# A two-block layer on one core: routing from the unscaled residual, choices by counted ranks, and places of two expert pairs at a time

## The chip, the cores and the metric

The kernel runs on one core of a Trainium2 chip. The metric is the device time of one execution in microseconds (us). TensorE is called PE here, VectorE DVE, ScalarE ACT, GpSimd POOL and SyncE SP; SP issues the weight transfers.

## What is computed

Two blocks on 256 tokens of 1024 fp32 values. The first is an attention layer with a PEER feed-forward part; the change does not touch it. The second is a parallel mixer, a cross-attention to 256 memory rows (weights w_q, w_kv, w_o), a hierarchical mixture of experts and a final norm:

```
def second_block(x, mem, ...):
    x = x + parallel_mixer(rms_norm_2(x, mix_norm[l]), ..., w_out[l])
    x = x + memory_cross_attention(rms_norm_2(x, xattn_norm[l]), rms_norm_2(mem, mem_norm[l]), w_q[l], w_kv[l], w_o[l])
    x = x + hierarchical_moe(rms_norm_2(x, ffn_norm[l]), ...)
    return rms_norm_2(x, final_norm)

def hierarchical_moe(h, w_group, b_group, w_expert, b_expert, w_gate, w_up, w_down):
    g_prob = softmax(t @ w_group + b_group)                     # 4 groups
    g_p, g_idx = lax.top_k(g_prob, 1)
    e_logits = (t @ w_expert + b_expert).reshape(-1, 4, 4)      # 4 experts in each
    e_logits = take_along_axis(e_logits, g_idx[:, :, None], axis=1)[:, 0]
    e_p, e_idx = lax.top_k(softmax(e_logits), 2)
    weights = g_p * e_p / sum(e_p)
    for e in range(16):
        hid = silu(t @ w_gate[e]) * (t @ w_up[e])
        out = out + combine[:, e:e + 1] * (hid @ w_down[e])
```

## The kernel before

Tokens stand in two halves of 128 on the partitions (`xs[0]`, `xs[1]`); `c` is the half. Dense products are made of high and low parts: `unit` (L198, L199) loads a weight tile `raw` and splits it into `whi` (ACT) and `wlo` (DVE), and `mm3` (L206 to L209) multiplies three of the four combinations.

**Cross-attention.** `add_out(yT, w_out2)` ends the mixer, adds to the residual, normalizes it and transposes it; `evac` writes the transposed rows as high and low parts `hq` (L289, L290). w_q, the attention per head, then w_o in two column blocks of 512 (`tok_block`, four units each). The last two units of the second block are done first for half 0, then for half 1 (`tail`).

**Routing.** Behind w_o's second block each half is added (L1239), squared and summed (ACT), scaled by rstd and the gain row into `xl` (L331), transposed (L303), copied to `hT` (L1300) and multiplied with the 20 routing columns (L1303). `split_chunk` (L225, L226) makes `xnh`, `xnl` of `xl`. From the logits `lg` a chain of small DVE operations finds the best group, the best two experts in it (by maxima, with ties broken by rank), and the weights. `M` is the 0/1 table of token to expert. Five matmuls with triangular and all-ones tables (L1377 to L1381) count the tokens ahead of each in its expert, and their totals.

**Places.** Each expert has 64 places. `one_hots` compares the position with 0 to 63 and so makes `Pm`, tokens by places; `gather` multiplies `xnh`, `xnl` with `Pm` and copies the result to `XT` (features by places), 512 places of eight experts at once: one half before the experts, the other (`late`) after the first pair's up and gate products. `back` transposes `Pm` to `PT`, `place_weights` gives each place its weight `cw`.

**Experts.** Two experts at a time, eight pairs `j`. `up_gate` takes eight loads of 1 MB (w_gu), four for the gate, four for up; `down` four (w_dn). `wide` (L1435) issues each load on SP's queue into the ring pool `rawm` of MOE_RAW slots, in which the tiles of w_q and w_o (512 KB each) stand before. SP issues in the order of the program; a load waits until its slot has been read. `to_tokens` puts the outputs back to tokens. If an expert has more than 64 tokens, the whole is repeated for the rest under `If`, by the total `toti` loaded into registers (L1548).

PSUM has four banks `acc` and four `aux`. Outside the listed places the order on the engines is a scheduler's.

Of the kernel before, what the change touches and what calls it, by code (L numbers as in the profile page):

```python
# [9 lines left out]
F32 = mybir.dt.float32  # L10
F32R = mybir.dt.float32r
I32 = mybir.dt.int32
# [10 lines left out]
MOE_RAW = 10  # L23
# [47 lines left out]
def pack(a):  # L71
# [61 lines left out]
    r["ffn"] = _rows(a["ffn_norm_2"][0])  # L133
# [12 lines left out]
def build(tc, I, out):  # L146
# [12 lines left out]
    with es:  # L159
# [201 lines left out]
        xd = dramp.tile([2, 128, D], F32, name="xd")  # L361
# [731 lines left out]
        with ExitStack() as ph:  # L1093
            stream(es, 0, 3, 3)
# [138 lines left out]
            def add_out(aT, src, gain=None, then=None):  # L1233
                tt = Turned(pair("l"))
                for nb in range(2):
                    sl = slice(nb * 512, (nb + 1) * 512)
                    pss = tok_block(aT, src[nb], 8, tail=nb == 1)
                    for c in range(2):
                        V.tensor_add(xs[c][:, sl], pss[c], xs[c][:, sl])  # L1239
                        if nb == 1:  # L1240
                            tt.chunk(xs[c], c, gain)
                            if then is not None:
                                then(tt, c)
                return tt
# [7 lines left out]
            hq = hl_tiles(qp, 8, "hq")  # L1252
# [33 lines left out]
            ffn = tp.tile([128, D], F32, name="ffn", tag="ffn", bufs=1)  # L1286
            SY.dma_start(ffn, I["ffn"])
            wr = qp.tile([128, 160], F32, name="wr")
            br = qp.tile([128, 20], F32, name="br")
            SY.dma_start(wr, I["w_route"])  # L1290
            SY.dma_start(br, I["b_route"])
            lg = small(40, "lg", bufs=1).rearrange("p (a b) -> p a b", a=2)
            hT = qp.tile([128, 8, T], F32, name="hT3", tag="qT")

            def logits(tt, c):
                cs = slice(c * 128, (c + 1) * 128)
                if c == 1:
                    xhl.append(split_chunk(tt.xn[0])[0])
                for q, ps in enumerate(tt.pss):
                    last = S.copy(hT[:, 2 * q:2 * q + 2, cs], ps.rearrange("p (a t) -> p a t", a=2)[:, :, cs])  # L1300
                pl = acc()
                for k in range(8):
                    PE.matmul(pl[:, 0:20], hT[:, k, cs], wr[:, k * 20:(k + 1) * 20], start=k == 0, stop=k == 7)  # L1303
                if c == 0:
                    V.tensor_add(lg[:, c], pl[:, 0:20], br)
                    return
                st["behind"] = (last, st["behind"][1])
                hl, last = split_chunk(tt.xn[1])
                xhl.append(hl)
                with tc.issue_after(last.ins):  # L1310
                    V.tensor_add(lg[:, c], pl[:, 0:20], br)

            xhl = []
            tt = add_out(oT, I["w_o"], ffn, logits)


        with ExitStack() as ph:
# [6 lines left out]
            xn = tt.xn  # L1324
            for c in range(2):
                G.dma_start(xd[c], xn[c])

            rank = mp.tile([128, 4], F32, name="rank")
            for i in range(4):
                V.memset(rank[:, i:i + 1], 4.0 - i)  # L1330
            rk = rank[:, None, :].to_broadcast([128, 2, 4])

            def bc4(m):
                return m.unsqueeze(2).to_broadcast([128, 2, 4])

            def first_max(p, name):
                m = small(2, name + "v")
                V.tensor_reduce(m, p, axis=AX.X, op=OP.max)
                oh = mp.tile([128, 2, 4], F32, name=name)
                V.tensor_tensor(oh, p, bc4(m), op=OP.is_equal)  # L1340
                V.tensor_mul(oh, oh, rk)
                r = small(2, name + "r")
                V.tensor_reduce(r, oh, axis=AX.X, op=OP.max)
                V.tensor_tensor(oh, rk, bc4(r), op=OP.is_equal)
                return oh, m

            def exps(x, m, name):
                p = mp.tile([128, 2, 4], F32, name=name)
                V.tensor_sub(p, x, bc4(m))
                S.activation(p, p, AF.Exp)  # L1350
                return p

            oh, gmax = first_max(lg[:, :, 0:4], "goh")
            gex = exps(lg[:, :, 0:4], gmax, "gex")
            gz = small(2, "gz")
            sel = mp.tile([128, 2, 4, 4], F32, name="sel")
            for c in range(2):
                V.tensor_mul(sel[:, c], lg[:, c, 4:20].rearrange("p (g e) -> p e g", g=4),
                             oh[:, c, None, :].to_broadcast([128, 4, 4]))
            el = mp.tile([128, 2, 4], F32, name="el4")  # L1360
            V.tensor_reduce(el, sel, axis=AX.X, op=OP.add)
            o1, m1 = first_max(el, "eo1")
            ex = exps(el, m1, "ex")
            ex2 = mp.tile([128, 2, 4], F32, name="ex2")
            V.scalar_tensor_tensor(ex2, o1, -4.0, ex, op0=OP.mult, op1=OP.add)
            o2, p2 = first_max(ex2, "eo2")
            V.tensor_add(o1, o1, o2)
# [222 lines left out]
```

## Time and profile before

| | |
|---|---|
| median of 3 runs | 1531.72 us (1527.82 to 1536.29) |
| profiled execution, own time | 1528.59 us |
| its span from first to last instruction | 1526.8 us |
| mean granted clock of PE | 0.942 of 2.4 GHz |
| PE busy over the span | 1255.9 us (82%) |
| DVE / ACT / POOL busy | 1028.4 / 498.5 / 412.4 us |
| moved by DMA | 493.17 MB, mean 323 GB/s |
| expert loads | 96 of 1024 KB, 19.9 us from issue to landing in the middle |

The shares of busy time are means over stages with different limits; the stage of the change is the last 340 us, and there single timelines are read.

### The profile page before, as it was taken

To read this page: it belongs to the slowest core of one execution; us is meant where nothing else is said; L and a number is where in the kernel's file an instruction comes from. 1 tells how busy PE (TensorE), PEld (TensorE's weight loads), DVE (VectorE), ACT (ScalarE), POOL (GpSimd) and SP (SyncE) were. 2 spreads that over 40 slices of the span, in tenths; PEclk is the share of its full clock that TensorE was granted. 3 is DMA by queue.
4 is the path that set the end of the run, shared out by engine and by line. 5 is a ranking of instruction groups with operands and counts; after the bars stand their busy time and mean duration, and the time that the engine had idled before them with its cause. 6 is when DMAs were issued, how large, how long until landed. Compare 5 with 4: busy or idle time off the path is not lost. (4 is left out here: it accounts for less than half of the span.)

```text
span 1526.8 us, 16025 instructions
## 1 busy us (share of the span) xinstructions
PE 1255.9 (82%) x5260; PEld 772.5 (51%) x5260; DVE 1028.4 (67%) x2132; ACT 498.5 (33%) x1001; POOL 412.4 (27%) x306
## 2 busy tenths in 40 slices
PE   7999999999898656666666656767999998998886
PEld 7878787778664222222222222224998875432222
DVE  6899877776878888888988888765896643100002
ACT  5555445754222222222122222213663532100001
POOL 0022000100455666556456565640000000000000
PEclk9999999999999998778899988899999997999999
DMA  8955876364889999999999999996436553999996
GB/s 330 352 204 190 266 275 207 111 247 180 336 354 421 421 420 421 420 420 422 420 421 421 420 420 421 420 421 236 165 111 235 182 207 127 369 420 420 419 420 247
DMA packets 86347, 493.17 MB, mean 323 GB/s; under 512 B 9712, under 2 KB 12528, under 8 KB 39920
## 3 DMA queue, kind: packets, MB, share of 16 engines
q0 software_dynamic: 37152, 269.50, 42.6%
q1 hardware_dynamic: 47088, 219.94, 38.7%
q10 hardware_dynamic: 2016, 2.62, 0.5%
q8 instruction: 44, 0.72, 0.2%
q14 instruction: 47, 0.39, 0.1%
HBM read 487.83 MB, written 4.19 MB: 322 GB/s over the span
## 5 line engine op out<-in xcount | busy, mean ns | idle before, releaser
L981 PE MATMUL acc<-uv,dg 128*128 128x512 f32 x784 | 418.0, 683 | 195.1 <-ACT dg L979 194.9
L944 POOL DMA_INDIRECT uv<-in_uv_dram,ei x256 | 368.7, 1440 | 285.6 <-DMA uv<-in_uv_dram,ei 115.0
L954 DVE CUSTOM_DVE_ANT_0 junk<-uv,h 128x1024 f32<-128x1024 f32 x256 | 313.0, 1223 | 111.1 <-DMA uv<-in_uv_dram,ei 109.3
L981 PEld LDWEIGHTS acc<-uv,dg 128*128 128x128 f32 x784 | 160.7, 215 | 445.4 <-ACT dg L979 277.0
L317 POOL TENSOR_TENSOR rstd<-ms,neghalf 128x1 f32<-128x1 f32 (+3 forms) x38 | 40.2, 1058 | 783.0 <-DVE ms L315 782.9
L199 DVE TENSOR_TENSOR wlo<-raw,whi 128x1024 fp32r<-128x1024 f32 x144 | 174.6, 1219 | 42.8 <-ACT whi L198 37.7
L198 ACT CAST whi<-raw 128x1024 fp32r<-128x1024 f32 x144 | 150.8, 1052 | 122.7 <-PE acc L207 49.0
L959 ACT ACTIVATE ga<-dots 128x2 f32<-128x2 f32 x128 | 26.0, 203 | 382.8 <-DVE dots L954 382.7
L1449 PE MATMUL aux<-raw,XT 128*64 128x512 f32 x512 | 117.6, 599 | 10.5 <-DMA raw<-in_w_gu_dram 10.5
L979 ACT ACTIVATE dg<-ident,wts 128x128 f32<-128x128 f32 x196 | 71.0, 395 | 104.9 <-DVE wts L964 101.9
L206 PE MATMUL acc<-whi,hTh 128*128 128x512 f32 (+1 forms) x240 | 96.6, 405 | 2.2 <-ACT whi L198 1.6
L1456 DVE SCALAR_TENSOR_TENSOR hid<-aux,cw,sgt 128x512 f32<-128x512 f32 x8 | 6.0, 750 | 136.0 <-PE aux L1449 136.0
L207 PE MATMUL acc<-whi,hTl 128*128 128x512 f32 (+1 forms) x240 | 93.4, 392 | 0.0
L1449 PEld LDWEIGHTS aux<-raw,XT 128*64 128x64 f32 x512 | 33.8, 136 | 86.0 <-issue 55.3
L973 DVE SCALAR_TENSOR_TENSOR xl<-uv,wts,xl 128x1024 f32<-128x1024 f32 x58 | 74.5, 1285 | 2.1
L1473 PE MATMUL aux<-raw,hTm 128*64 128x512 f32 x256 | 60.1, 600 | 12.5 <-DMA raw<-in_w_dn_dram 12.0
L209 PE MATMUL acc<-wlo,hTh 128*128 128x512 f32 (+1 forms) x240 | 64.7, 389 | 2.3 <-DVE wlo L199 2.3
L866 PE MATMUL aux<-h2T,uv 128*128 128x256 f32 (+1 forms) x288 | 56.8, 356 | 0.0
L277 DVE TENSOR_TENSOR yl<-aux,yh 128x512 fp32r<-128x512 f32 x16 | 11.1, 691 | 67.4 <-ACT yh L276 67.4
L391 DVE SCALAR_TENSOR_TENSOR ada<-raw,csil,ada 128x1024 f32<-128x1024 f32 x42 | 53.7, 1278 | 0.3 <-DMA raw<-in_w_ada_dram 0.2
L866 PEld LDWEIGHTS aux<-h2T,uv 128*128 128x128 f32 x288 | 49.7, 190 | 7.4 <-issue 1.9
L206 PEld LDWEIGHTS acc<-whi,hTh 128*128 128x128 f32 x240 | 46.0, 192 | 14.5 <-ACT whi L198 3.2
(426 smaller groups left out, 1947.5 us busy)
## 6 DMA issues: line engine op xcount, KB each, us to landing
raw<-in_w_gu_dram SPq DMA_DIRECT2D x64, 1024.0 KB, 19.9
raw<-in_w_dn_dram SPq DMA_DIRECT2D x32, 1024.0 KB, 19.9
raw<-in_w_ada_dram SPq DMA_DIRECT2D x48, 512.0 KB, 4.6
raw<-in_w_qk_dram SPq DMA_DIRECT2D x28, 512.0 KB, 4.6
raw<-in_w_gl_dram SPq DMA_DIRECT2D x16, 512.0 KB, 4.3
uv<-in_w_query_dram SPq DMA_DIRECT2D x8, 1024.0 KB, 9.5
raw<-in_w_out_dram SPq DMA_DIRECT2D x16, 512.0 KB, 4.3
raw<-in_w_v_dram SPq DMA_DIRECT2D x14, 512.0 KB, 4.5
```

Of the source, the lines that this page charges most:

```text
L198: S.copy(hi, raw)
L199: V.tensor_sub(lo, raw, hi.bitcast(F32))
L206: PE.matmul(ps, a[0], b[0], start=first, stop=False)
L207: PE.matmul(ps, a[late], b[1 - late], start=False, stop=False)
L209: PE.matmul(ps, a[1 - late], b[late], start=False, stop=last)
L866: PE.matmul(ps[:, half * w:(half + 1) * w], wq[h][:, j:j + 128], h2T[:, k, cs], start=k == 0, stop=k == 7)
L944: G.indirect_dma_start(out=t, out_offset=None, in_=I["uv"], in_offset=bass.IndirectOffsetOnAxis(ap=ei[:, c, h, k:k + 1], axis=0))
L954: V.tensor_tensor_reduce(junk, fetched[h, c, k][:, 0:D], h2[c], scale=1.0, scalar=0.0, op0=OP.mult, op1=OP.add, accum_out=dots[:, c, h, k: ...
L973: V.scalar_tensor_tensor(part[c], t, w, part[c], op0=OP.mult, op1=OP.add)
L979: S.mul(dg, ident, w)
L981: PE.matmul(vacc[c, i], dg, t[:, i * 512:(i + 1) * 512], start=c not in first, stop=(h, k) == (7, 14 + c))
L1449: PE.matmul(ps[e * 64:(e + 1) * 64], XT[:, k, (2 * j + e) * 64:(2 * j + e + 1) * 64], w[:, (2 * e + i) * 512:(2 * e + i + 1) * 512], start ...
```

## The change

In words: (1) the routing weights are multiplied by the gain column once; the residual itself is transposed and multiplied with them, and rstd is applied to the 20 logits. The first 512 columns of the residual are transposed inside w_o's second block, their logits too. (2) Choices: each logit in a row of four counts those that are greater (or equal, for those ahead of it); rank below 1 for the group and below 2 for the expert gives `M`. The weights are computed later. (3) `xhl`, the high and low parts of the normalized tokens, takes the memory of `hq`; the DRAM copy `xd` goes. (4) `places(q)` works on two pairs (256 places); q = 0 before the experts, 1 to 3 after the downs of pairs 0, 2 and 4. (5) MOE_RAW is 11. (6) The totals move behind the experts. (7) From w_o's second block to the first gather the order on PE, DVE and ACT is the program's, and on PE to the end of the experts.

```diff
-MOE_RAW = 10
+MOE_RAW = 11
...
-            stream(es, 0, 3, 3)
+            stream(ph, 0, 3, 3)
...
-            hq = hl_tiles(qp, 8, "hq")
+            hqp = es.enter_context(pool("hqp", side="right"))
+            hq = hl_tiles(hqp, 8, "hq")
             tt.evac(hq, col("xattn_norm"), None, tp)
             st["raw"] = es.enter_context(pool("rawm", MOE_RAW, side="right"))
...
+            V.tensor_mul(wr, wr, gcol.unsqueeze(2).to_broadcast([128, 8, 20]))
...
+            xhl = [[t.rearrange("p k t -> p (k t)")[:, c * D:(c + 1) * D] for t in hq] for c in range(2)]
...
+            def logits_out(c):
+                V.scalar_tensor_tensor(lg[:, c], pls[c], rs[c], br, op0=OP.mult, op1=OP.add)
+            def highs(c):
+                S.activation(xhl[c][0], xs[c], AF.Copy, scale=rs[c])
+            def lows(c):
+                V.scalar_tensor_tensor(xhl[c][1], xs[c], rs[c], xhl[c][0].bitcast(F32), op0=OP.mult, op1=OP.subtract)
+            for c, po in enumerate(tok_block(oT, I["w_o"][0], 8)):
+                add(c, 0, po)
+                squares(c, 0)
+                turned(c, 0, turn_half(c, 0), S.copy)
+            given.enter_context(tc.manual_schedule(engines={ET.PE, ET.DVE, ET.Activation}))
+            last_o = tok_gen(oT, I["w_o"][1], 8, 512, po.extend, tail=True)
+            for u in range(2):
+                next(last_o)
+            for c in range(2):
+                logits(c, 0)
+            for _ in last_o:
+                pass
...
+            V.tensor_tensor(gt, others_, own, op=OP.is_gt)
+            V.tensor_tensor(ge, others_, own, op=OP.is_ge)
+            V.copy_predicated(gt.rearrange("p r a b -> p r (a b)"), tri[:, None, :].to_broadcast([128, 10, 16]),
+                              ge.rearrange("p r a b -> p r (a b)"))
+            rank = mp.tile([128, 2, 20], F32, name="rank")
+            V.tensor_reduce(rank.rearrange("p c (r f) -> p (c r) f", f=4), gt, axis=AX.X, op=OP.add)
+            oh = mp.tile([128, 2, 4], F32, name="oh")
+            V.tensor_scalar(oh, rank[:, :, 0:4], 0.5, None, op0=OP.is_lt)
...
-            PE.matmul(ps[:, 0:16], before, Mf[:, 0], start=True, stop=True)
-            PE.matmul(ps[:, 16:32], before, Mf[:, 1], start=True, stop=False)
+            PE.matmul(ps[:, 0:32], before, M.rearrange("p c g e -> p (c g e)"), start=True, stop=False)
             PE.matmul(ps[:, 16:32], ones, Mf[:, 0], start=False, stop=True)
-            PE.matmul(ps[:, 32:48], ones, Mf[:, 0], start=True, stop=False)
-            PE.matmul(ps[:, 32:48], ones, Mf[:, 1], start=False, stop=True)
+            lows(0)
...
+            def gather(q):
+                hs = slice(q * 256, (q + 1) * 256)
+                pss = [aux() for _ in range(4)]
+                for p in range(2):
+                    for k, c in ([(k, c) for c in range(2) for k in range(8)] if p == 0 else
+                                 [(k, c) for k in range(8) for c in range(2)]):
+                        PE.matmul(pss[k // 2][:, k % 2 * T:(k % 2 + 1) * T], xhl[c][p][:, k * 128:(k + 1) * 128],
+                                  Pm[:, c, hs], start=c == 0 and p == 0 and k % 2 == 0,
+                                  stop=c == 1 and p == 1 and k % 2 == 1)
...
-                        if which == 0 and u == 1:
+                        if which == 0 and u == 2:
                             between()
...
+                    if j == 0:
+                        place_weights(0)
+                        back(range(2))
...
+                    if j % 2 == 1 and j < 6:
+                        q = (j + 1) // 2
+                        places(q)
+                        place_weights(q)
+                        back(range(2 * q, 2 * q + 2))
```

The order on PE from w_o's last matmuls (L209, changed: L210) to the first expert matmuls (L1449, changed: L1486) was, with the transposes L303, the logits L1303, the counts L1377 to L1381, the gather L1404, and `back` and `place_weights` as L1419 and L1427:

```order
L209 MATMUL acc<-wlo,oTh 128x512 x4
L303 MATMUL aux<-ident,xl 128x128 x8
L1303 MATMUL acc<-wr,hT_8522 128x20 x8
L303 MATMUL aux<-ident,xl 128x128 x8
L1303 MATMUL acc<-wr,hT_8522 128x20 x8
L1377 MATMUL aux<-M,before 128x16
...
L1404 MATMUL aux<-Pm,xnh 128x512
L1404 MATMUL aux<-Pm,xnl 128x512
...
L1419 MATMUL aux<-ident,Pm 128x128 x8
L1427 MATMUL aux<-cx,Pm 128x2 x8
L1449 MATMUL aux<-raw,XT 64x512 x32
```

and is now, with the logits L1328, the transposes of the residual L1313, the counts L1410 and L1411, the gather L1433, `place_weights` L1464 and `back` L1455:

```order
L1328 MATMUL aux<-wr,xT_8523 128x20 x8
...
L210 MATMUL acc<-wlo,oTh 128x512 x4
L1313 MATMUL aux<-ident,x_74 128x128 x4
L1313 MATMUL aux<-ident,x_75 128x128 x4
L1328 MATMUL aux<-wr,xT_8523 128x20 x8
L1410 MATMUL aux<-M,before 128x32
L1411 MATMUL aux<-M,ones 128x16
L1433 MATMUL aux<-Pm,hqh 128x256 x16
L1433 MATMUL aux<-Pm,hql 128x256 x16
L1486 MATMUL aux<-raw,XT 64x512 x12
L1464 MATMUL aux<-cx,Pm 128x2 x4
L1455 MATMUL aux<-ident,Pm 128x128 x4
```

Half of the transposes and logits moved into w_o; `place_weights` and `back` moved behind the third load of the first pair.

The second gather on PE stood between the gate and the up loads of pairs 0 and 1 (32 matmuls of 512 columns, of which two rows are shown):

```order
L1449 MATMUL aux<-raw,XT 64x512 x32
L1404 MATMUL aux<-Pm,xnh 128x512
L1404 MATMUL aux<-Pm,xnl 128x512
...
L1419 MATMUL aux<-ident,Pm 128x128 x8
L1427 MATMUL aux<-cx,Pm 128x2 x8
L1449 MATMUL aux<-raw,XT 64x512 x8
```

and is now the first of three blocks, behind pair 0's down (L1473, changed: L1510):

```order
L1510 MATMUL aux<-raw,hTm 64x512 x16
L1433 MATMUL aux<-Pm,hqh 128x256 x16
L1433 MATMUL aux<-Pm,hql 128x256 x16
L1464 MATMUL aux<-cx,Pm 128x2 x4
L1455 MATMUL aux<-ident,Pm 128x128 x4
L1486 MATMUL aux<-raw,XT 64x512 x12
```

It moved from behind eight loads to behind twenty, with half the columns.

At w_q's start the order on ACT was, with the sums of squares L325, the splits whi of w_q's tiles L198 and the evacuations hqh L289:

```order
L325 ACTIVATE xl,ssq_8064<-x_76 128x512
L198 CAST whi<-raw 128x1024 x2
L289 ACTIVATE hqh<-aux,cols 128x256 x4
L198 CAST whi<-raw 128x1024
L289 ACTIVATE hqh<-aux,cols 128x256 x4
```

and is now (L326, L199 and L290):

```order
L326 ACTIVATE xl,ssq_8063<-x_75 128x512
L290 ACTIVATE hqh<-aux,cols 128x256 x7
L199 CAST whi<-raw 128x1024 x2
L290 ACTIVATE hqh<-aux,cols 128x256
```

Seven of the eight evacuations now stand ahead of w_q's first split.

## Rows read from the trace of the kernel before

**Rows 1.** Stretches: length, busy (instructions) of PE, PEld, DVE, ACT, POOL; PEclk, DMA share, GB/s
```profile
1195.00:1250.00 55.00, 54.97 (x319) 47.81 (x318) 27.82 (x51) 25.14 (x49) 0.00 (x0) 1.00 0.64 224
1260.00:1275.00 15.00, 9.13 (x38) 8.51 (x37) 8.86 (x46) 2.93 (x8) 0.53 (x1) 0.50 0.18 70
1275.00:1285.00 10.00, 9.97 (x54) 8.06 (x55) 3.83 (x8) 4.29 (x7) 0.00 (x0) 0.96 0.01 2
1305.00:1320.00 15.00, 14.97 (x83) 7.19 (x84) 1.78 (x6) 2.52 (x5) 0.00 (x0) 1.00 0.77 287
1320.00:1500.00 180.00, 158.76 (x692) 50.60 (x690) 13.54 (x19) 14.72 (x25) 0.00 (x0) 1.00 1.01 420
```

**Rows 2.** Waits of PE from 1240 us: total us, times, longest
```profile
PE aux L1473 <- DMA raw<-in_w_dn_dram: 12.0, 20, 1.3
```

**Rows 3.** Timeline of SP: start us, us, operation, count
```profile
1163.37 3.76 SPq L179 DMA_DIRECT2D raw<-in_w_q_dram  x8
...
1205.74 40.76 SPq L1435 DMA_DIRECT2D raw<-in_w_gu_dram  x10
...
1286.54 8.91 SPq L1435 DMA_DIRECT2D raw<-in_w_gu_dram  x6
```

**Rows 4.** Timeline of PE, w_o's end to the experts; idle before in brackets
```profile
1251.75 1.07 PE L209 MATMUL acc<-wlo,oTh 128*128 128x512 f32 x4
...
1269.30 0.58 PE L1377 MATMUL aux<-M,before 128*128 128x16 f32 x2 [4.65 <-issue]
...
1272.81 0.79 PE L1404 MATMUL aux<-Pm,xnh 128*128 128x512 f32 x1 [1.22 <-DVE Pm L1392]
...
1275.10 0.63 PE L1404 MATMUL aux<-Pm,xnl 128*128 128x512 f32 x1
1275.53 0.48 PE L1404 MATMUL aux<-Pm,xnh 128*128 128x512 f32 x1
...
1281.44 0.39 PE L1404 MATMUL aux<-Pm,xnl 128*128 128x512 f32 x1
1281.67 1.28 PE L1419 MATMUL aux<-ident,Pm 128*128 128x128 f32 x8
1282.79 1.84 PE L1427 MATMUL aux<-cx,Pm 128*128 128x2 f32 x16
1284.56 5.80 PE L1449 MATMUL aux<-raw,XT 128*64 128x512 f32 x26
```

**Rows 5.** Timeline of DVE in the routing
```profile
1252.69 1.29 DVE L331 SCALAR_TENSOR_TENSOR xl<-x,rstd,ffn 128x1024 f32<-128x1024 f32 x1 [0.73 <-POOL rstd L317]
1253.90 0.68 DVE L1239 TENSOR_TENSOR x<-acc,x 128x512 f32<-128x512 f32 x1
...
1264.69 0.18 DVE L1311 TENSOR_TENSOR lg<-acc,br 128x20 f32<-128x20 f32 x1 [0.66 <-PE acc L1303]
...
1272.06 2.50 DVE L1392 TENSOR_TENSOR Pm<-iota,pos 128x512 fp32r<-128x512 f32 x4
```

**Rows 6.** Timeline of PE around the second half's gather
```profile
1298.45 0.50 PE L1404 MATMUL aux<-Pm,xnh 128*128 128x512 f32 x1
...
1308.88 3.65 PE L1449 MATMUL aux<-raw,XT 128*64 128x512 f32 x16
```

**Rows 7.** Timelines at w_q's start, PE and then ACT
```profile
1181.92 1.07 PE L209 MATMUL acc<-wlo,yTh 128*128 128x512 f32 x4
...
1188.41 0.78 PE L206 MATMUL acc<-hqh,whi 128*128 128x256 f32 x2
...
1187.58 1.69 ACT L289 ACTIVATE hqh<-aux,cols 128x256 fp32r<-128x256 f32 x4 [0.78 <-PE aux L303]
1189.17 1.04 ACT L198 CAST whi<-raw 128x1024 fp32r<-128x1024 f32 x1
```

**Rows 8.** The tile raw from 1130 to 1215 us: from issue to landing
```profile
DMA to landing us min/median/max: 3.4/4.3/11.6
```

**Rows 9.** Timeline of PE at the last down
```profile
1512.11 1.94 PE L1473 MATMUL aux<-raw,hTm 128*64 128x512 f32 x8 [0.50 <-SPq L1552]
```

More of the change, by code (lines that the diff above doesn't have):

```diff
@@ L1313, in build @@
-            xhl = []
-            tt = add_out(oT, I["w_o"], ffn, logits)
+            xT = qp.tile([128, 8, T], F32, name="xT3", tag="qT")
+            sq = [small(2, f"ssqr{c}", bufs=1) for c in range(2)]
+            slot = small(64, "slot", bufs=1)
+            V.tensor_scalar(slot, iota[:, 0:64], -1024.0, None, op0=OP.add)
+            xhl = [[t.rearrange("p k t -> p (k t)")[:, c * D:(c + 1) * D] for t in hq] for c in range(2)]
+            pls = {}
+            tri = small(16, "tri", I32, bufs=1)
@@ new lines, in build, with add, turn_half, squares @@
+            SY.dma_start(tri, I["tri"])
+            def add(c, nb, po):
+                sl = slice(nb * 512, (nb + 1) * 512)
+                V.tensor_add(xs[c][:, sl], po, xs[c][:, sl])
+            def turn_half(c, nb):
+                pt = aux()
+                for i in range(4):
+                    k = 4 * nb + i
+                    PE.transpose(pt[:, i * 128:(i + 1) * 128], xs[c][:, k * 128:(k + 1) * 128], ident)
+                return pt
+            def squares(c, nb):
+                sj = tp.tile([128, 512], F32, name="sj", tag="sj")
+                S.activation(sj, xs[c][:, nb * 512:(nb + 1) * 512], AF.Square, accum_out=sq[c][:, nb:nb + 1])
@@ new lines, in turned, with logits, scale @@
+            def turned(c, nb, pt, copy):
+                copy(xT[:, 4 * nb:4 * nb + 4, c * 128:(c + 1) * 128], pt.rearrange("p (a t) -> p a t", a=4))
+            def logits(c, nb):
+                if nb == 0:
+                    pls[c] = aux()[:, 0:20]
+                cs = slice(c * 128, (c + 1) * 128)
+                for k in range(4 * nb, 4 * nb + 4):
+                    PE.matmul(pls[c], xT[:, k, cs], wr[:, k], start=k == 0, stop=k == 7)
+            rs = []
+            def scale(c):
+                ssq = small(1, "ssq")
+                V.tensor_add(ssq, sq[c][:, 0:1], sq[c][:, 1:2])
+                rs.append(rstd_of(ssq, 1, D))
@@ L1317, in build @@
+            add(1, 1, po[1])
+            turned(0, 1, pt, S.copy)
+            pt = turn_half(1, 1)
+            squares(1, 1)
+            logits(0, 1)
+            turned(1, 1, pt, V.tensor_copy)
+            scale(1)
+            logits(1, 1)
+            highs(0)
+            for c in range(2):
+                logits_out(c)
+            highs(1)
         with ExitStack() as ph:
@@ L1347, in exps @@
[L1347 to L1367, printed above, removed]
+            rows4 = lg.rearrange("p c (r f) -> p (c r) f", f=4)
+            gt = mp.tile([128, 10, 4, 4], F32, name="gt")
@@ new lines, in build @@
+            for c in range(2):
+                one_hots(c, 0)
+            lows(1)
+            st["filled"] = gather(0)
+            m4 = mp.tile([128, 10], F32, name="m4")
+            V.tensor_reduce(m4, rows4, axis=AX.X, op=OP.max)
+            ex = mp.tile([128, 2, 20], F32, name="ex")
+            ex4 = ex.rearrange("p c (r f) -> p (c r) f", f=4)
+            V.tensor_sub(ex4, rows4, m4.unsqueeze(2).to_broadcast([128, 10, 4]))
+            S.activation(ex, ex, AF.Exp)
+            given.close()
```

156 lines of the change are left out of this document (59 added, 97 removed).

## The prediction, made before the changed kernel was run

> **What bounds the kernel now.** I first read the stretches from the memory cross-attention to the end [rows 1]. The reader should look at two columns of them: PE busy and DMA share. From 1195 to 1250 us (w_q, attention, w_o) PE is busy 54.97 of 55 us, so there the bound is PE, and whatever is added to PE's list lengthens the stage. From 1275 to 1285 the DMA share is 0.01: nothing flows. From 1320 to 1500 the share is 1.01 at 420 GB/s while PE is busy 158.76 of 180 us: the expert weights are streamed as fast as they come and PE waits. The waits of PE say the same by name: the largest is 12.0 us for w_dn, in 20 short waits before single loads [rows 2]. A load is 1 MB (128 x 2048 x 4 bytes), so at 420 GB/s one takes 2.5 us.
>
> The timeline of SP says why nothing flows from 1275 to 1285 [rows 3]: ten w_gu loads are issued ahead, into the ten slots of the ring, from 1205.74 to 1246.5; the eleventh goes out at 1286.54. The one PE row that explains this is the first L1449 at 1284.56 [rows 4]: a slot becomes free only when the expert matmuls have read it. So the end of the kernel is the first release, plus 86 remaining loads of 2.5 us, plus every gap in that stream, plus a tail of the last 8 matmuls (1512.11 [rows 9]) and the final norm. A change is worth what it moves of these: the time of the first release, the count of loads behind it, the gaps.
>
> Between w_o's end on PE (1251.75 + 1.07 = 1252.82) and 1284.56 lie 31.7 us [rows 4]. In them PE is idle or on small matmuls, the clock is granted at 0.50 from 1260 to 1275 [rows 1], and the chain is DVE's: the scaled copy of 1.29 us per token half, transposes, logits, the last lg at 1264.69, 29 small routing operations up to 1269.30, five matmuls of counts, positions, four compares Pm in 2.50 us, then 32 gather matmuls, 8 transposes and 8 weight matmuls [rows 4, 5]. The gap is the second half's gather with its transposes, which stands on PE between loads from 1298.45 to 1308.88, 10.4 us [rows 6]; the DMA share from 1305 to 1320 is 0.77 for that [rows 1], because at that time few loads were in flight and no slot was returned.
>
> **The change, part by part.** I call w_o's end on PE E.
>
> Added to w_o's second column block, where PE has no room: 8 transposes and 8 logits matmuls of the first 512 columns. Eight transposes take 1.1 us (1281.67 to 1282.79, 8 rows of L1419 [rows 4]); eight logits matmuls are 16 PE records of a matmul with few columns, and 16 such records of L1427 took 1.8 us (1282.79 to 1284.56 [rows 4]). Sum +3.0 us on E.
>
> The chain after E: residual add 0.68 [rows 5]; 4 transposes 0.6; copy out of PSUM, as wide as the add, 0.7; 4 logits matmuls 0.9; lg 0.2; four hand-overs between engines at about 0.2. That is E + 3.9. The routing is then 8 operations in place of 29. No row of before has a 160-element compare: the lower bound is a small operation, which I put at 0.2 us (29 of them took the 4.4 us up to 1269.30, and some overlap), the upper one half of a 512-wide Pm (2.50 / 4) and a fixed part, 0.36. I take 1.9 us for all 8 (bounds 1.6, all 0.2 apart, and 2.9, all 0.36). Two count matmuls in place of five: 1269.30 to about 1271.6 for five is 0.46 each, so 0.9. Position 0.2, two Pm of half the width 0.7, hand-overs 0.3. First gather matmul at E + 7.9. The STT of 1.28 us that makes the low part of half 0 lies beside the count matmuls, that of half 1 beside the first 16 gather matmuls, which read high parts only; if this cover were gone, it would cost 1.3 each. A gather matmul of 512 columns is 0.43 apart at half clock (1275.10 to 1275.53) and 0.23 at full clock (1281.44 to 1281.67 [rows 4]); half as wide, 0.215 and 0.117. All 32 at half clock take 6.9 us, all at full clock 3.8; I take 5.0, since in before 2.7 us passed (1272.81 to 1275.53) until the faster pitch came. No transposes and no weight matmuls stand before the first expert matmul any more. First expert matmul at E + 12.9 against E + 31.7: −18.8 us.
>
> Moved without being named in the diff's words: the first w_q load. The hq tiles move to a pool of their own ahead of the ring on the right side, the ring gets one slot more, and the first slot then lies over memory that w_out2's stage still uses. In the built program that load waits for w_out2's last matmul (1181.92 + 1.07 = 1183.0 [rows 7]); in before it went out at 1163.37 [rows 3]. SP is in order, so all eight w_q loads go with it, and the scheduler puts seven hqh evacuations ahead of the first whi on ScalarE. Landing took 3.4 us at least, 4.3 in the middle, 11.6 at most [rows 8]; a whi is 1.04 [rows 7]. Lower bound 0: ScalarE is with the evacuations until about 1190.5 anyway. Upper bound 1183.0 + 11.6 + 1.04 − 1188.41 (first w_q matmul [rows 7]) = +7.3. I take +2.5: seven evacuations of 0.42 from 1187.58 on [rows 7], then whi, puts the first matmul at 1191.6, 3.1 late, of which the matmuls then win some back, as in before they started in fits.
>
> So the first release moves by 3.0 + 2.5 − 18.8 = −13.3 us.
>
> Ring of 11: one load fewer behind the first release, 85 in place of 86: −2.5 us. This holds as the eleventh load finds about 20 us without traffic before it.
>
> Places in quarters: the blocks on PE between loads become 32 matmuls of 256 columns (3.8), 4 weight matmuls (8 records, 0.9), 4 transposes (0.6), and about 1 us of waiting for yl and PSUM, b = 6.3 us each, three of them; the first comes after pair 0's down, when six or more loads are in flight. Six loads are 15 us of traffic, so the stream doesn't stop: the gap of before goes, 15 × (1 − 0.77/1.01) = −3.5 us (bounds 0 and −4). PE pays for it from its slack: 95 loads × 1.74 us (8 loads from 1284.56 to 1298.45 [rows 4, 6]) + 8 turns × 0.6 (four transposes) + 6 to_tokens × 1.9 (eight matmuls of 512 columns, 0.23 apart) + 1.6 for pair 0 = 182.7 + 3b, against 3.7 (the first load's matmuls, and about 2 until transfers flow) + 85 × 2.5 = 216 us for the stream. PE takes over as the bound from b = 11 on.
>
> Costed at nothing: the removed xd copies (POOL's queue, nobody waits), the totals and their register load moved to the end (on PE two small matmuls behind the first load of the last down, on SP behind the last weight load), the exps and weights (under the gather; needed only at pair 0's hid). The new small tri load is issued early. If the totals did stand in the tail they would cost about 1 us.
>
> One rule weighs against the price of a load. The rows show 420 GB/s over 180 us [rows 1]. The Trainium skill, "DMA: Bandwidth & Descriptors", section "Where 436 GB/s comes from", says that HBM to SBUF transfers are bound by the HBM side at about 358 GB/s per core; by that a load would take 2.9 us and the sum would be 0.4 us better. The trace does not agree here, and the rows decide.
>
> **Sum.** −13.3 − 2.5 − 3.5 = −19.3 us against the profiled execution's 1528.59: 1509.3. The median of the three runs shown, 1531.72, is 3.1 above that execution, so on that footing 1512.4. I say 1511.
>
> **The rivals.**
> R1, the late w_q loads cost their upper bound: the eight loads start together and the first is slow to land; +4.8 on the forecast, 1516. For it: up to 11.6 us seen; against it: the median of 4.3, and that only one to two loads are needed at once. Chance 0.12.
> R2, the other side: PE becomes the bound through the three blocks. Place: after the downs of pairs 0, 2 and 4. Price 3 × (b − 11) us; it is slower than before from 3 (b − 11) > 19.3, b = 17.5. Against it: the double block of before took 10.4 [rows 6]; for it: a block now waits for yl, Pm and four PSUM banks in turn. At b = 19 it is 1511 + 24 = 1535. Chance 0.03.
> R3, PE stays at 1.2 GHz through routing, gather and into the experts, because the new chain keeps PE idle until E + 7.9 and the gather is short: +1.9 in the gather, +0.9 in logits, +1.7 on the first expert load, and +1 at w_q's start: +5, 1516. For it: 0.50 from 1260 to 1275 [rows 1]; against it: 0.96 in the next ten us, after only 2.7 us of gather at half speed. The Trainium skill, "TensorE: Matmul & The Clock Gate", section "What's actually happening", says that the throttled state is the default and activity releases it, which would go with R3; the trace agrees as to the drop. Chance 0.12.
> R4, the chain does not shorten: something (a PSUM bank of the four, the tri tile, a slot of the hq pool) holds the gather until where it was. Then −18.8 falls away, and +5.5 − 6.0 stays: 1528 to 1531. Against it: each of these is released before w_o ends in the listed order. Chance 0.05.
> The forecast: 0.68.
>
> **How the numbers follow.** The likeliest case goes from 1504 (no loss at w_q, full clock in the gather, the profiled run's footing) to 1516. R1 and R3 together reach 1521. The range 1502 to 1522 leaves out R4, R2 and their mixtures, under 0.2. A measurement of this kernel tells about 0.5%, 7.7 us; faster by more than that means under 1524. Forecast, R1 and R3 are (0.92, less 0.03 for mixtures): faster 0.89; R4 and mixtures: same 0.08; R2: slower 0.03.
>
> **What would show it.** First w_q load on SP at about 1183 and the first w_q matmul 2 to 4 us later than 1188.4; w_o's last matmul at about 1258; first gather matmul 8 us and first expert matmul 13 us behind it, near 1271; eleven w_gu loads before it, then a DMA share of 1.0 without a dip until 1490; three groups of 32 narrow matmuls, each with what follows under 7 us on PE; last 8 matmuls near 1493. It is wrong if PE shows no waits for loads in the middle (R2), if the share dips after the first downs, or if the gap from w_o's end to the experts is over 16 us.

## The result and the profile after

The changed kernel takes 1508.76 us (median of 4 runs, 1507.45 to 1509.14) against 1529.77 us of the kernel before (4 runs beside it): ratio 0.986, 95% interval 0.9837 to 0.9882. The profiled execution has a span of 1505.6 us, 21.2 less than before's 1526.8. The forecast of 1511 lies 2 us off.

Both profiles can be compared from w_out2's last product on; what lies ahead of it is the same work and moved by 0.75 us between them. The marks of the two, in us:

| | before | changed | difference | forecast |
|---|---|---|---|---|
| w_out2's end to the first products of keys and q | 13.41 | 15.41 | +2.0 | +2.5 |
| from there to w_o's end E | 56.42 | 59.80 | +3.4 | +3.0 |
| E to the first gather matmul | 19.99 | 7.41 | −12.6 | −12.1 |
| first gather matmul to first expert matmul | 11.75 | 5.80 | −6.0 | −6.8 |
| first expert matmul to first load into a freed slot | 1.98 | 1.98 | 0 | 0 |
| that load to the end of the last expert matmul | 227.51 | 219.19 | −8.3 | −6.0 |
| from there to the end of the span | 12.75 | 12.27 | −0.5 | 0 |
| sum, from w_out2's end | 343.81 | 321.86 | −21.95 | −19.4 |

(The forecast's column adds to −19.4, the prediction's sum to −19.3; that is rounding.) The rows behind them. The first products of keys and q, in before (L1267) and in the changed kernel (L1266):

```profile
1196.40 0.60 PE L1267 MATMUL aux<-kT,qT 128*128 128x256 f32 x2
...
1199.15 0.60 PE L1266 MATMUL aux<-kT,qT 128*128 128x256 f32 x2
```

PE's timeline of the changed kernel (start, duration, line, operation, count, idle before) from w_o to the experts, and the first block of places between the loads:

```profile
1251.51 1.86 PE L1328 MATMUL aux<-wr,xT 128*128 128x20 f32 x16
1253.21 0.49 PE L207 MATMUL acc<-whi,oTh 128*128 128x512 f32 x1
...
1257.88 1.07 PE L210 MATMUL acc<-wlo,oTh 128*128 128x512 f32 x4
...
1264.52 0.61 PE L1410 MATMUL aux<-M,before 128*128 128x32 f32 x2 [2.27 <-issue]
...
1266.36 3.75 PE L1433 MATMUL aux<-Pm,hqh 128*128 128x256 f32 x16 [0.83 <-DVE Pm L1422]
1269.91 2.32 PE L1433 MATMUL aux<-Pm,hql 128*128 128x256 f32 x16
1272.16 5.37 PE L1486 MATMUL aux<-raw,XT 128*64 128x512 f32 x24
...
1309.02 1.12 PE L1433 MATMUL aux<-Pm,hqh 128*128 128x256 f32 x6
...
1315.35 5.37 PE L1486 MATMUL aux<-raw,XT 128*64 128x512 f32 x24 [0.24 <-ACT PT L1457]
```

L1328 ahead of w_o's last matmuls is the first half of the logits: 1.7 us until the next row, in a stage in which PE is full. Against [rows 4] the reader should see three stretches: from the end of w_o (1257.88 + 1.07) to the counts at 1264.52, 5.6 us, where it took 16.5 in before (1252.82 to 1269.30); the gather, whose first 16 matmuls take 3.55 us and the last 16 only 2.25; and nothing between the gather and 1272.16, the first expert matmul. The block from 1309.02 to 1315.35 is the 6.3 us that the forecast called b. The timeline of SP, which answers to [rows 3]:

```profile
1183.81 3.75 SPq L180 DMA_DIRECT2D raw<-in_w_q_dram  x8
...
1205.77 45.02 SPq L1472 DMA_DIRECT2D raw<-in_w_gu_dram  x11
...
1274.14 8.82 SPq L1472 DMA_DIRECT2D raw<-in_w_gu_dram  x5
```

Eleven loads are issued ahead of the experts. Then the first freed slot is filled at 1274.14, 12.4 us sooner than at 1286.54. The w_q loads go out at 1183.81, right behind w_out2's last product, whereas before they went out 20 us ahead of it. On PE that looks so, to be read with [rows 7]:

```profile
1182.67 1.07 PE L210 MATMUL acc<-wlo,yTh 128*128 128x512 f32 x4
...
1191.72 0.58 PE L207 MATMUL acc<-hqh,whi 128*128 128x256 f32 x1 [3.03 <-ACT whi L199]
```

The stretches, to be read with [rows 1] (length, busy of PE, PEld, DVE, ACT, POOL with counts, clock, DMA share, GB/s):

```profile
1265.00:1270.00 5.00, 4.17 (x20) 4.09 (x20) 2.71 (x5) 0.00 (x0) 0.00 (x0) 0.50 0.05 20
...
1275.00:1280.00 5.00, 5.00 (x30) 2.37 (x28) 0.93 (x4) 0.37 (x1) 0.00 (x0) 1.00 0.97 326
...
1310.00:1315.00 5.00, 4.64 (x40) 4.37 (x38) 2.22 (x6) 1.96 (x5) 0.00 (x0) 1.00 1.01 421
...
1320.00:1480.00 160.00, 148.70 (x706) 58.11 (x704) 17.21 (x32) 17.47 (x32) 0.00 (x0) 1.00 1.01 419
```

The clock is at 0.50 in the five us of the gather's first part, as it was from 1260 to 1275 in before. From 1275 on the DMA share is 1.0, also in the stretch of the first block (1310 to 1315); the 0.77 of before is gone. PE's waits for loads, which were 12.0 us for w_dn [rows 2], have shrunk too:

```profile
PE aux L1510 <- DMA raw<-in_w_dn_dram: 5.0, 9, 0.7
```

That is under half of before's: PE, which has the blocks of places now in this time, is later at the loads. At the end it is PE that comes last:

```profile
1481.23 1.94 PE L1510 MATMUL aux<-raw,hTm 128*64 128x512 f32 x8 [0.57 <-DMA raw<-in_w_dn_dram]
...
1487.96 5.37 PE L1510 MATMUL aux<-raw,hTm 128*64 128x512 f32 x24
```

The last wait for a load is at 1481.23; the last down, of which 1487.96 is the second to fourth load, runs without one, where before's last load was waited for until 1512.11 [rows 9].

### The profile page after: what moved, and what is told of

Read it like the earlier page. It is cut to its first block, busy times and chain, and to the rows that moved or that the text cites. A ratio compares the mean times of both kernels' runs of the same rounds, so it can differ in the third digit from the quotient of the medians.

```text
span 1505.6 us, 16139 instructions
## 1 busy us (share of the span) xinstructions
PE 1257.6 (84%) x5322; PEld 778.5 (52%) x5322; DVE 1029.3 (68%) x2128; ACT 500.8 (33%) x1003; POOL 411.0 (27%) x304
## 5 line engine op out<-in xcount | busy, mean ns | idle before, releaser
L981 PE MATMUL acc<-uv,dg 128*128 128x512 f32 x784 | 430.1, 702 | 185.3 <-ACT dg L979 185.3
L981 PEld LDWEIGHTS acc<-uv,dg 128*128 128x128 f32 x784 | 166.2, 222 | 442.3 <-ACT dg L979 264.8
L199 ACT CAST whi<-raw 128x1024 fp32r<-128x1024 f32 x144 | 150.9, 1053 | 126.2 <-PE acc L208 51.5
L1486 PE MATMUL aux<-raw,XT 128*64 128x512 f32 x512 | 114.9, 597 | 6.4 <-DMA raw<-in_w_gu_dram 4.3
L1486 PEld LDWEIGHTS aux<-raw,XT 128*64 128x64 f32 x512 | 35.0, 137 | 78.9 <-issue 61.7
L210 PE MATMUL acc<-wlo,hTh 128*128 128x512 f32 (+1 forms) x240 | 64.6, 389 | 2.2 <-DVE wlo L200 2.2
L1510 PE MATMUL aux<-raw,hTm 128*64 128x512 f32 x256 | 58.7, 598 | 5.1 <-DMA raw<-in_w_dn_dram 5.0
L210 PEld LDWEIGHTS acc<-wlo,hTh 128*128 128x128 f32 x240 | 43.5, 188 | 12.0 <-DVE wlo L200 2.7
```

What stands on the lines that cost most here:

```text
L199: S.copy(hi, raw)
L210: PE.matmul(ps, a[1 - late], b[late], start=False, stop=last)
L981: PE.matmul(vacc[c, i], dg, t[:, i * 512:(i + 1) * 512], start=c not in first, stop=(h, k) == (7, 14 + c))
L1486: PE.matmul(ps[e * 64:(e + 1) * 64], XT[:, k, (2 * j + e) * 64:(2 * j + e + 1) * 64], w[:, (2 * e + i) * 512:(2 * e + i + 1) * 512], start ...
```

## The experiments

The 1180 us ahead of the stage differ between executions and chips by several us (runs of the kernel before: 1524 to 1537), so edits worth 2 us are read in two ways: by medians beside the changed kernel on one chip where there is one, and by the profile from w_out2's end, as in the table above. The changed kernel was profiled three times: 321.86 us, 323.79 (`changed_again`) and 321.78 (`changed_third`). What made the second longer is the clock: w_o's end comes 1.35 us later behind w_out2's, and the gather lasts 6.38 us in place of 5.80 (the low stretches at w_q's start are shown below).

**The late load.** Edit:

```diff
+            st["raw"] = es.enter_context(pool("rawm", MOE_RAW, side="right"))
             hqp = es.enter_context(pool("hqp", side="right"))
             hq = hl_tiles(hqp, 8, "hq")
             tt.evac(hq, col("xattn_norm"), None, tp)
-            st["raw"] = es.enter_context(pool("rawm", MOE_RAW, side="right"))
```

> The ring is allocated ahead of hq on the right side, so that its first slot no longer lies over memory of w_out2's stage; nothing else differs from the changed kernel (1508.8). My theory (the late w_q loads cost PE time that nothing hides): w_q's first load goes out near 1163 to 1168 again, the first w_q matmul is 2 to 3 us earlier than 1191.7, and the whole is 2.0 to 2.6 us shorter, 1506.2 to 1506.8. Rival (the delay is absorbed before the experts, since PE waits there anyway): the start moves, the time stays at 1508.8 within 0.5.

1506.38 us median (before beside it 1532.21; ratio 0.9841, 0.9816 to 0.9866). The first w_q load goes out 19.6 us ahead of w_out2's end again, and the first w_q matmul comes 4.95 us behind that end in place of 7.98. But the products of keys and q come only 0.5 sooner, w_o ends 1.0 sooner, and from w_out2's end to the end it is 321.47, 0.4 less than the changed kernel. PE's rows at w_out2's end, the first products of keys and q, and w_o's end:

```profile
1185.36 1.07 PE L210 MATMUL acc<-wlo,yTh 128*128 128x512 f32 x4
...
1201.33 0.59 PE L1266 MATMUL aux<-kT,qT 128*128 128x256 f32 x2
...
1259.53 1.07 PE L210 MATMUL acc<-wlo,oTh 128*128 128x512 f32 x4
```

The median lies in the theory's range, but the changed kernel was not run beside it; the profile's 0.4 lies in the rival's. So it was run again beside the changed kernel.

> The changed kernel once more, beside the others of this group on one chip, since the 1180 us ahead of the stage differ between chips by more than the edits are worth. 1506 to 1512; from the last product with w_out2 to the end of the span 321.9 us in its first profile, here 321.5 to 323.

1509.63 us median; 323.79 from w_out2's end.

> The ring ahead of hq once more, beside the changed kernel. In its first profile PE's first product with w_q came 3.0 us sooner, but the clock stood at 0.50 for some 7 us of w_q's start against some 5 in the changed kernel and 3 in the kernel before, and only 0.4 us were left at the end. My theory: the cost of the late load is 2 to 3 us at full clock and the clock's low stretch differs between executions, so the median of several runs is 1.0 to 2.6 us below that of the changed kernel. Rival: w_q's start is set by the clock and the evacuations whatever the load does, so the medians agree within 0.7 us.

1507.22 us median, 2.4 below the changed kernel beside it, in the theory's range, while the intervals of the two ratios (0.9838, 0.9808 to 0.9869; 0.9858, 0.9829 to 0.9886) overlap. From w_out2's end 321.83. The stretches of low clock at w_q's start, in before, in the changed kernel's first profile, in `changed_again` and in this profile:

```profile
1187.00:1190.00 3.00, 2.68 (x12) 2.38 (x11) 3.00 (x5) 2.42 (x5) 0.00 (x0) 0.50 0.31 57
...
1188.00:1195.00 7.00, 3.97 (x22) 3.73 (x21) 6.23 (x11) 5.85 (x11) 0.00 (x0) 0.54 1.02 414
...
1190.00:1200.00 10.00, 7.47 (x35) 7.07 (x34) 6.88 (x11) 5.98 (x11) 0.00 (x0) 0.50 1.03 404
...
1192.00:1199.00 7.00, 6.05 (x29) 5.66 (x28) 5.84 (x12) 3.60 (x8) 0.00 (x0) 0.52 0.59 164
```

At w_q's start seven us pass at 0.52 here and at 0.54 in the changed kernel's first profile, ten at 0.50 in `changed_again`, three in before. Between profiles with the same seven us low, w_o ends 1.0 us sooner with the early load (74.2 against 75.2 behind w_out2's end): 0.5 of it up to the first products of keys and q, 0.5 from there to w_o's end (59.27 in both swapped profiles, 59.80 in the changed kernel). So the late load costs about 1.0, and ten us at the low clock in place of seven another 1.35 (76.56 in `changed_again`); the length differs between executions of one kernel. Whether the late load makes a long stretch likelier, these profiles can't tell.

**The slots.** Edit: MOE_RAW = 10 in the changed kernel.

> The changed kernel with ten slots in place of eleven. My theory (the end is the first release plus 2.5 us for each load behind it): one load more behind the release, the first release where it was, +2.0 to +2.5 us, 1510.8 to 1511.3. Rival (at the end PE and no longer the stream sets the time, since in the changed kernel the last down runs without a wait): +0 to +0.8, at most 1509.6.

1514.25 us median (before 1532.21; ratio 0.9882, 0.9862 to 0.9901). The first release is where it was (15.19 behind E in both); from it to the last expert matmul 222.18 us in place of 219.19, +3.0. The rival falls. Half a microsecond over the bound of 2.5 is not explained.

A twelfth slot in the output tile's memory, with the output built in XT:

```diff
+MORE = 1
...
+            st["rawx"] = ph.enter_context(pool("rawx", MORE))
...
+                raw = st["raw" if n < MOE_RAW else "rawx"].tile([128, 2048], F32, name="raw", tag="raw")
...
-            o = [tp.tile([128, D], F32, name="of", tag="of") for c in range(2)]
+            o = [XT[:, c] for c in range(2)]
```

> The changed kernel with a twelfth slot in the memory that the output tile had (the output is built in XT, which is free by then). My theory: one load fewer behind the first release, the release where it was, 2.3 to 3.0 us shorter than the changed kernel (the step from ten slots to eleven was 3.0 from the release to the last product in the profiles). Rival (the stretch without traffic ahead of the release is already used, or PE sets the end): 0 to 0.8 us.

1509.27 us median, beside 1509.63 of the changed kernel: no gain in the whole. The profile says why: from the release to the last expert matmul 216.80 us, 2.4 less, as the theory says, and 2.0 of it are lost behind, in the final norm. The timeline of DVE there, and the same row of the changed kernel (L1617):

```profile
1495.33 2.64 DVE L1563 TENSOR_TENSOR x<-acc,x 128x512 f32<-128x512 f32 x4
1500.05 1.23 DVE L1621 CUSTOM_DVE_ANT_0 XT<-x 128x1024 f32<-128x1024 f32 x1 [2.08 <-PEq L1609]
...
1497.46 1.23 DVE L1617 CUSTOM_DVE_ANT_0 of<-x 128x1024 f32<-128x1024 f32 x1 [0.22 <-DVEq L1605]
```

The square sum waits 2.08 us for PE's queue at the `If` (L1609), whose body reads the tile XT in which the output now lies; the changed kernel waits 0.22 there. So the twelfth slot confirms the price of a slot, and the loss was the experiment's own.

**The places between the loads.** Edit: the three blocks stand behind the first eight expert loads.

```diff
-                    if j % 2 == 1 and j < 6:
-                        q = (j + 1) // 2
+                    for q in range(1, 4) if j == 0 else ():
                         places(q)
                         place_weights(q)
                         back(range(2 * q, 2 * q + 2))
```

> The changed kernel, but the three blocks of places stand one after the other behind the first eight expert loads, where the second half's gather stood in the kernel before. My theory (a block between loads is free only while enough loads are in flight; eight issued behind the first release carry the stream for 20 us): eight loads from 1274.1 flow until about 1296, PE is back at the expert matmuls at about 1303 to 1304 (three blocks of 5.3 to 6.3), the DMA share falls to 0 for 10 to 12 us, and the whole is 10 to 12 us longer, 1519 to 1521. Rival (PE's slack and the eleventh slot hide where the blocks stand): no stretch under 0.9 DMA share, 1508.8 to 1511.

1523.02 us median (before 1532.21; ratio 0.9951, 0.9932 to 0.9969). PE's blocks and the DMA shares around them:

```profile
1287.80 2.43 PE L1433 MATMUL aux<-Pm,hqh 128*128 128x256 f32 x16
...
1294.57 3.36 PE L1433 MATMUL aux<-Pm,hqh 128*128 128x256 f32 x16 [1.18 <-DVE Pm L1422]
...
1308.10 5.37 PE L1486 MATMUL aux<-raw,XT 128*64 128x512 f32 x24 [0.24 <-ACT PT L1457]
```

```profile
1285.00:1296.00 11.00, 9.80 (x66) 7.31 (x63) 3.97 (x10) 2.26 (x5) 0.00 (x0) 0.96 1.01 422
...
1298.00:1310.00 12.00, 10.58 (x82) 8.99 (x83) 5.79 (x16) 4.52 (x10) 0.00 (x0) 0.98 0.00 0
```

The blocks last from 1287.80 to 1308.10, 20.3 us, longer than taken, since the second and the third wait 1.2 us for their Pm and the clock fell in the second. The eight loads carried the stream to 1296.5, and from 1298 to 1310 it stood at zero. From the release to the last expert matmul 234.67 us, +15.5 where 10 to 12 were expected: the blocks end 4 us later than taken. That the stream stops when the loads in flight run out holds; the size was short by 3.5.

**The choices.** Edit: `first_max`, `sel`, `exps` and the 0/1 tables of the kernel before in place of `gt`, `ge`, the ranks and `oh`.

> The changed kernel with the choices found by maxima as in the kernel before (the weights computed late as in the changed one). My theory: from the last lg to the end of M 4.2 to 4.8 us in place of 2.0, the first release 2.3 to 2.9 us later and the whole as much, 1511.1 to 1511.7. Rival 1 (the first gather is paced by the low parts and the clock, not by the choices): +0 to +1. Rival 2 (a longer idle stretch of PE keeps the clock low into the gather): the gather takes over 6.3 us in place of 5.8 and the whole is +3.2 or more.

1514.65 us median (before 1532.21; ratio 0.9883, 0.9864 to 0.9902). PE's timeline:

```profile
1273.36 0.61 PE L1436 MATMUL aux<-M,before 128*128 128x32 f32 x2 [5.07 <-issue]
```

The counts come 8.37 us behind E in place of 5.57, +2.8, and the first release +3.0: the theory's size, and rival 1 falls. The gather is 6.0 us long in place of 5.8, so rival 2 does not hold either. The whole is +4.0 from w_out2's end, 1.1 over the theory's bound; this lies behind the release (219.95 and a tail of 12.67) and is not explained.

**Work inside w_o.** Edit: the loop over `logits(c, 0)` stands behind w_o, ahead of `logits(0, 1)`.

> The changed kernel beside the others of this group. From the last product with w_out2 to the end 321.9 and 323.8 us so far; 321.5 to 324.

1507.36 us median; 321.78 from w_out2's end.

> The changed kernel, but the 8 logits matmuls of the first 512 columns stand behind w_o and the transposes. My theory (PE has no room inside w_o, so what moves there from behind it is paid in full): w_o ends 1.8 us sooner, the first release is where it was within 0.5 us, the whole within 0.7 us of the changed kernel. Rival (work inside w_o is partly hidden): the whole 1 to 2 us longer.

1512.34 us median, beside 1507.36 of the changed kernel (ratios 0.9876, 0.985 to 0.9903, and 0.9853, 0.9826 to 0.988). PE's timeline:

```profile
1264.29 3.65 PE L1328 MATMUL aux<-wr,xT 128*128 128x20 f32 x32
...
1277.91 5.37 PE L1486 MATMUL aux<-raw,XT 128*64 128x512 f32 x24
```

w_o ends 1.7 us sooner, the logits behind it are 32 records in place of 16, and the first expert matmul is 1.77 later behind E. From w_out2's end 321.84 against 321.78. By the profile it is neutral, as the theory says. The medians are 5 us apart the other way, with intervals that overlap; in the two profiled executions 5.4 us lie ahead of w_out2's last product (its end at 1189.56 against 1184.12), where the edit changes nothing.

**The clock in the gather.** Edit:

```diff
+            idle = acc()
+            for _ in range(8):
+                PE.matmul(idle, xhl[0][0][:, 0:128], xhl[0][0][:, 0:512], start=True, stop=True)
             ps = aux()
             PE.matmul(ps[:, 0:32], before, M.rearrange("p c g e -> p (c g e)"), start=True, stop=False)
...
             lows(1)
+            for _ in range(4):
+                PE.matmul(idle, xhl[0][0][:, 0:128], xhl[0][0][:, 0:512], start=True, stop=True)
             st["filled"] = gather(0)
```

> The changed kernel with 8 matmuls of 512 columns, whose result nobody reads, between the logits and the count matmuls, and 4 more ahead of the first gather, so that PE isn't idle there. My theory (half of the first gather ran at 1.2 GHz because PE stood idle for 2.3 and 0.8 us ahead of it): granted clock over 0.95 from the logits to the experts, first gather 3.7 to 4.0 us in place of 5.8, the whole 1.7 to 2.4 us shorter than the changed kernel. Rival (the clock falls all the same, since the idle stretch behind w_o's end has already been): the extra matmuls run 0.43 apart, hold up the count matmuls by over 1 us, and the whole is 0 to 2 us longer.

1505.20 us median, 4.4 below the changed kernel beside it (ratio 0.9829, 0.9802 to 0.9856). PE's timeline:

```profile
1260.67 2.07 PE L1412 MATMUL acc<-hqh 128*128 128x512 f32 x8
...
1263.53 1.17 PE L1576 MATMUL acc<-hqh 128*128 128x512 f32 x4
1264.80 2.15 PE L1437 MATMUL aux<-Pm,hqh 128*128 128x256 f32 x16
1266.79 2.04 PE L1437 MATMUL aux<-Pm,hql 128*128 128x256 f32 x16
1268.77 5.37 PE L1490 MATMUL aux<-raw,XT 128*64 128x512 f32 x24
```

The added matmuls (L1412, L1576) fill the two idle stretches at 0.24 apart, each half of the gather takes 2.0 us, and from the first gather matmul to the first expert matmul it is 3.97 in place of 5.7 to 6.4. The first release is 13.2 behind E in place of 15.1 to 15.7. With the idle stretches filled, the clock held, as the theory said. The whole is another matter: from w_out2's end this profile takes 321.79 us, as much as two of the changed kernel's three. Its w_q start was one with ten us at the low clock (w_o ends at 76.52, in `changed_again` at 76.56), and its tail is 13.04 in place of 12.27. Against `changed_again` it is 2.0 less. The other part of the 4.4 us between the medians is not shown to come from the edit; in the two profiled executions 4.9 us lie ahead of w_out2's end (1181.01 against 1185.91).

**All three.** The early load, the busy PE, and a twelfth slot whose memory does not bring PE into the tail (output in place in `xs`, leftovers in bf16, `gt` and `ge` in XT).

> The changed kernel with the ring ahead of hq, the idle PE kept busy ahead of the first gather, and a twelfth slot, whose memory comes from the output being made in place (the sums of squares write bf16 leftovers nobody reads) and two comparison tables lying in XT. My theory: the three gains add, 1 to 2 + 2 to 2.5 + 2.4: from the last product with w_out2 to the end 315.5 to 317.5 us, 5 to 7 us below the changed kernel. Rival (the gains overlap, since with an earlier release PE sets the end): 318.5 or more.

1502.32 us median, beside 1507.36 of the changed kernel (ratio to before 0.9821, 0.9794 to 0.9849). From w_out2's end 315.87, 5.9 less than `changed_third`: release 86.84 behind w_out2's end in place of 90.24, 216.72 from there to the last expert matmul in place of 219.29, tail 12.31. The gains add in this profile, with seven us at the low clock at w_q's start in both.

> The kernel before this in the list, with 9 more matmuls nobody reads between the two halves' transposes at w_q's start, where PE waits 2 us for DVE. My theory (w_q's start ran 3 to 7 us at 1.2 GHz because of these waits): no stretch at 0.50 from w_out2 to w_o, and 1.5 to 3 us less than all_three from the last product with w_out2 to the end. Rival (the start is paced by ACT and DVE, which make hq and the split weights): under 0.7 us less.

1500.12 us median (ratio 0.9805, 0.978 to 0.983). At w_q's start the clock stays at 1.00, and w_o ends 72.24 us behind w_out2's end in place of 73.62: 1.4 won. But only 0.6 is left from w_out2's end (315.29), by these rows:

```profile
1269.10 3.66 PE L1418 MATMUL acc<-hqh 128*128 128x512 f32 x8
1272.60 0.30 PE L1420 MATMUL aux<-M,before 128*128 128x32 f32 x2
```

```profile
1193.70:1207.70 14.00, 12.19 (x83) 10.40 (x82) 10.80 (x19) 9.23 (x17) 0.56 (x1) 1.00 0.36 120
...
1270.00:1272.00 2.00, 2.00 (x6) 1.52 (x6) 1.86 (x7) 0.25 (x1) 0.00 (x0) 0.50 0.97 403
```

This time the clock fell as the added matmuls began (0.60 from 1269.0 to 1269.5, with no idle stretch of PE of more than 0.35 us since w_o): the eight took 3.5 us instead of 1.9 and held the counts up by 1.1 us (6.65 behind E against 5.57). So an idle stretch is not the only way in which the clock is lost there. Work that nobody reads protects the clock, and costs when the clock falls all the same. Between this kernel and `all_three` the medians (2.2 apart, intervals that overlap) decide nothing.

## Why the prediction was right

The mechanism was the one forecast: the first release came as much sooner as the chain behind w_o got shorter, and the stream behind it lost one load and its gap. The near number owes something to terms that cancel.

*The frame* (end = first release + loads behind it + gaps + tail) held: ten, eleven and twelve slots moved the time from the release to the last expert matmul to 222.2, 219.2 and 216.8 us, 2.4 to 3.0 a slot, against 2.5 taken.

*w_o lengthened* by 3.4 against 3.0 (the prediction's two parts, 1.1 and 1.8, add to 2.9). About 0.5 of it goes with the late load: with the pools swapped the stretch is 59.27, 2.85 more than in before. It was paid in full: by the profile, with the logits moved back behind w_o the end stood where it was. What the move into w_o brought is thus nothing for the logits; transposes and copies were not tried alone.

*The chain behind E*: 13.2 us against 12.9. The routing has seven operations, not eight; with the hand-over they took 1.9 us from the last lg to the counts, as taken:

```profile
1262.36 0.24 DVE L1338 SCALAR_TENSOR_TENSOR lg<-aux,rstd,br 128x20 f32<-128x20 f32 x1 [0.81 <-PE aux L1328]
...
1264.16 0.26 DVE L1404 SCALAR_TENSOR_TENSOR M<-rank,oh 128x16 f32<-128x16 f32 x2
```

Against the maxima they are worth 2.8. The rest of the 18.5 us that the chain lost (the unscaled residual, the narrower gather, the transposes and weights moved behind the first loads) was not tried part by part; it is read from the two timelines. The gather was 5.8 against 5.0: the low clock reached over all of its first half, not 13 of 32 matmuls. Both ends given, 3.8 and 6.9, stand; `pe_kept_busy` reached 3.97. So R3 was there in part, in the gather and, as the next paragraph says, at w_q's start, not in the logits nor in the first expert matmuls, and the gather's term was off by 0.8. The Trainium skill, "TensorE: Matmul & The Clock Gate", section "HAM oscillation — how this bites in real kernels", advises restructuring a kernel of thin matmuls so that PE stays warm across its waits; `pe_kept_busy` agrees as to the gain, 5.7 to 6.4 us down to 3.97, though it fills the waits with matmuls that nobody reads.

*The late load* was there as read from the built program: the load at w_out2's end, the first w_q matmul 2.6 later behind it. As a cost of its own it was over-sized: 2.5 taken, about 1.0 by the swapped pools at the same clock. Of the +2.0 in the table only 0.5 is the load's. The other 1.5 stand in the swapped profiles too, whose load is as early as in before (14.90 and 14.97 against 13.41); there the clock is low for seven us, in before for three. That the clock is the cause is argued from this; R3 had priced it at 1 and the sum had left it out. So the over-sized load and the missing clock cancelled, which was luck. The upper bound, 7.3, adds to 7.2. R1 did not come.

*The stream* is the term with the largest error: 6.0 taken (2.5 + 3.5), 8.3 measured. The gap of 3.5 was taken from the DMA share of 1305 to 1320 alone. The stream's last microseconds show more. Stretches of the kernel before, columns as above:

```profile
1508.00:1509.00 1.00, 1.00 (x8) 0.42 (x6) 0.00 (x0) 0.00 (x0) 0.00 (x0) 1.00 0.57 238
1509.00:1510.00 1.00, 1.00 (x8) 0.26 (x6) 0.00 (x0) 0.00 (x0) 0.00 (x0) 1.00 0.12 49
1510.00:1511.00 1.00, 1.00 (x6) 0.29 (x4) 0.00 (x0) 0.00 (x0) 0.00 (x0) 1.00 0.08 33
1511.00:1512.00 1.00, 0.61 (x4) 0.00 (x0) 0.00 (x0) 0.00 (x0) 0.00 (x0) 1.00 0.02 8
```

and of the changed kernel:

```profile
1488.00:1489.00 1.00, 1.00 (x7) 0.43 (x8) 0.33 (x2) 0.00 (x0) 0.00 (x0) 1.00 0.67 279
1489.00:1490.00 1.00, 1.00 (x8) 0.31 (x6) 0.00 (x0) 0.00 (x0) 0.00 (x0) 1.00 0.32 131
1490.00:1491.00 1.00, 1.00 (x6) 0.29 (x4) 0.00 (x0) 0.00 (x0) 0.00 (x0) 1.00 0.06 25
```

In before the last pieces trail for three us from 1509, at shares of 0.12 and less, and PE got its last load at 1512.11; in the changed kernel it is two us, at 0.32 and 0.06, and PE's last load needed no wait. Added up to the end of the last expert matmul, the missing share is some 1.2 us less than in before. The other 1.1 of the 2.3 is not placed, and why the last pieces trailed less was not tried; with single profiles both stay open. The blocks of places were 6.3 us each, as taken, and R2 stayed away: in the whole of 1320 to 1480 PE was busy 148.7 of 160 us, so some 11 us of room are left there.

*The tail* gave 0.5 that was not in the sum.

R4 did not come. By the rows of the table the errors (w_o +0.4, gather +0.8, chain up to the gather −0.5, late load and clock −0.5, stream −2.3, tail −0.5) add to −2.6, the difference between −19.4 and −21.95.

## What to carry to other kernels

Where a ring of loads runs ahead of a stage that is bound by transfers, the end is the first freed slot plus the loads behind it, so what counts is how early the first consumer runs and how many slots stand ahead of it, and work between loads is free while the loads in flight outlast it: check that per place, since the same three blocks cost nothing spread and 15 us in a row. Work moved into a stage where the engine is already full is only moved, not hidden, as the logits here. A pool that changes sides can tie a transfer to another stage's last instruction; look in the built program at what the first load of a ring waits for.

## What had not been expected of the hardware

The clock's low stretch at w_q's start was 3 us long in one profile, 7 in most and 10 in others, of the same order of work, and w_o's end lay 1.35 us later with ten than with seven. Behind logits of 20 columns and an idle stretch of 2.3 us ahead of the counts, the first half of the gather ran at 1.2 GHz. Eight matmuls of 512 columns in that place kept 2.4 GHz in two profiles of three; in the third the clock fell as they began (0.50 from 1270 to 1272), some 3 us behind the end of w_o. A store into a tile that PE reads inside an `If` waited 2.08 us for PE to pass the branch.
